# First projection of a hybrid decoder layer: squares on ScalarE, a weight split in front of the norm, one activation table for logarithm and exponent

## The chip, the cores and the metric

The kernel runs on one core of a Trainium2 chip. A core has five engines that work side by side, each with its own queue of instructions in a fixed order: TensorE (PE, matmuls, with its weight loads listed as PEld), VectorE (DVE), ScalarE (ACT), GpSimd (POOL) and SyncE (SP, which here issues most of the data transfers). They wait for each other through semaphores. The metric is the device time of one execution in microseconds.

## The reference, cut to what matters

One decoder layer over 512 positions of width 1024, in float32. The part that the change touches is the first line of work: the norm of the input and the combined input projection.

```
def rms_norm(x, g):
    xf = x.astype(jnp.float32)
    y = xf * lax.rsqrt(jnp.mean(xf * xf, axis=-1, keepdims=True) + NORM_EPS)
    return (y * g.astype(jnp.float32)).astype(x.dtype)
...
    h = rms_norm(x, norm_mix[l])
    proj = h @ w_in[l]
    hq, hf, hi, hg, mq, mk, mv = jnp.split(proj, IN_SPLITS, axis=-1)
    o_hgrn = hgrn2_mixer(hq, hf, hi, hg, lb_table[l], hgrn_norm[l])
```

The columns hf are the forget logits of a gated recurrence (f = lb + (1 - lb) sigmoid(hf), and its logarithm is summed up within chunks), hi its inputs, hq its queries, hg an output gate; mq, mk and mv feed a block-sparse attention. Behind this come an output projection, a cross-attention to 256 memory tokens, and an MLP with a squared ReLU, each with its norm and residual.

## The kernel before, in words

The activations lie transposed: 1024 features as eight slices of 128 partitions, 512 positions along the free axis. The weights come in units of 128x1024 (512 KB), numbered in the order of use. A unit is loaded by SP into a raw tile (wr; three such buffers, so that a load waits until an earlier unit has been split), and then split into two parts of reduced precision: the upper part wh is a copy on ACT, the lower part wl the difference on DVE (split_unit, L266 to L269). Each product is then three matmuls: upper by upper, upper by lower, lower by upper.

The norm is not applied to x in front of the projection. x is scaled by the gain alone and split (xhi on ACT, xlo on DVE, split_x), and the factor 1/rms, which depends on the position only, is multiplied into the results: rb1 holds it along the free axis, rc1 (made from rb1 by small matmuls, nc) per partition.

The stretch of the change, in the order of the code. First the loads of x and of the four units of the forget projection hf, mixed (L482 to L491). Then a tiny logarithm of eps on ACT (L517). Then, slice by slice as data arrive, split_w (the four units' columns), split_x and square_x(k). square_x squares slice k, on ACT for even k and on DVE for odd k, and DVE adds the squares up in Sx (slices 0 to 3) and Sy (4 to 7) and at last both in Sx. Slice 0 enters hf unsplit, as xg0, so its split comes last (split_x(0), L569); it is needed by the next stage, hi.

The projection hf (L626 to L640) runs over the slices, and within a slice over the four units, into four accumulator banks. Of the norm, norm_rows, three parts are hung into it: at slice 5 the sums are split for the column sum (nrh on ACT, nrl on DVE) and lower_bounds is issued, which needs one small exponent (lbv); at slice 6 two matmuls with ones give the column sum nr, ACT makes rb1 from it as exp(-0.5 ln(.)) (rsqrt_of), and split_unit() splits unit 4, the first unit of hi. Then ev_f empties each of the four banks on DVE (Fz = hf times rb1), ACT takes the sigmoid, DVE scales it. The stage hi uses the same four banks.

Two things set the order of instructions. Up to L642 (and from L1248 on) they run on each engine as they are written. Between these lines the Tile scheduler orders them, by its own estimate of when each is ready and by the order of the code; there the code itself also interleaves side work (the heads' recurrences and attentions) by a table of estimated times, the class Pace. The logarithm, the exponent and the sigmoid need an activation table on ACT; the compiler puts a load in front of each that needs another table than the one present. A line nc.scalar.preload_act_table_set(name) asks for a set by name; the MLP has one at L1178.

## Time and profile before

| | |
|---|---|
| time, median of 3 runs | 752.73 us (750.14, 752.73, 753.45) |
| the profiled execution | 749.8 us, its span 748.0 us, granted TensorE clock 0.996 |
| busy: PE, DVE, ACT | 734.2, 545.8, 415.3 us |
| hf stage on PE | 5.28 to 29.9 us after the start |
| first matmul of hi | 32.50 us after the start |

The span is the time from the first to the last instruction in the profile. Times in the profile's rows are microseconds after its start. Nearly all of the kernel's instructions are issued through one helper, so they carry the line L115; the names of the tiles tell them apart. A name on the left of an arrow is what an instruction writes, those on the right are what it reads. In a timeline a row gives the start, the duration, the engine, the operation, and, in brackets, how long the engine stood idle before it and what it waited for; "x2" means that neighbouring equal instructions are merged into one row.

### The profile page before, as it was taken

Reading aid. Unit: us, or ns where it says so; the run is one execution under the profiler, and the core shown is the slowest. Engines: PE = TensorE matmul, PEld = TensorE weight load, DVE = VectorE, ACT = ScalarE, POOL = GpSimd, SP = SyncE. Lnnn points to the kernel's source line nnn. Section 1 sums busy time; section 2 is a strip of 40 time slices with the busy share of each in tenths; the row PEclk is TensorE's granted clock in tenths of the full one; section 3 lists DMA queues with packets and bytes.
Section 4 is the critical chain, followed back from the end, with each engine's and each line's share of the span. In section 5 each row is a group of like instructions: output and inputs, shape, how many; then the busy total and the mean of one; then the engine's idle time right before and its main releaser. Section 6 shows DMA issues by size and latency. Waiting matters only on the chain.

```text
span 748.0 us, 11991 instructions
## 1 busy us (share of the span) xinstructions
PE 734.2 (98%) x4702; PEld 662.4 (89%) x4702; DVE 545.8 (73%) x894; ACT 415.3 (56%) x636; POOL 49.4 (7%) x62
## 2 busy tenths in 40 slices
PE   9899999999999999999999999999999999999995
PEld 6688888777787998888888999999999999999995
DVE  5799744877776646677468788787879778878783
ACT  6684547334665554455355655555556554546562
POOL 1000000000011210011001011222100000000000
PEclk9999999999999999999999999999999999999998
DMA  9134334534679897459826488899986655545631
GB/s 312 50 130 152 113 113 141 182 128 142 169 201 253 206 291 286 141 125 275 285 104 141 109 236 217 226 216 236 236 205 236 199 191 177 191 147 173 218 117 57
DMA packets 45321, 137.03 MB, mean 183 GB/s; under 512 B 4528, under 2 KB 8880, under 8 KB 44624
## 3 DMA queue, kind: packets, MB, share of 16 engines
q1 hardware_dynamic: 35824, 110.64, 43.4%
q0 software_dynamic: 8960, 25.17, 18.8%
q8 instruction: 37, 0.61, 0.3%
q10 hardware_dynamic: 480, 0.45, 0.2%
q14 instruction: 20, 0.16, 0.1%
HBM read 134.15 MB, written 35.65 MB: 227 GB/s over the span
## 4 chain that ended last, share of the span: by engine, by line
PE 93%; ACT 3%; DVE 2%; DMA 1%; issue 1%; SPq 0%; DVEq 0%; ACTq 0%
PE X L115 24%; PE Y L115 15%; PE xo L115 7%; PE mkq L115 6%; PE xq L115 6%; PE wo L115 5%; PE Z L115 3%; PE hi L115 3%; PE hg L115 3%; PE mv L115 3%; PE hq L115 3%; PE memv L115 3%; PE memk L115 2%; PE xs L115 2%; PE a L115 1%; PE sc L115 1%
## 5 line engine op out<-in xcount | busy, mean ns | idle before, releaser
L115 ACT ACTIVATE wh<-wr 128x1024 fp32r<-128x1024 f32 x120 | 125.8, 1055 | 114.2 <-PE X L115 16.9
L115 DVE TENSOR_TENSOR wl<-wr,wh 128x1024 fp32r<-128x1024 f32 x120 | 146.0, 1221 | 43.0 <-ACT wh L115 28.5
L115 PE MATMUL X<-op,wh 128*128 128x256 f32 x512 | 92.7, 284 | 0.0
L115 PEld LDWEIGHTS X<-op,wh 128*128 128x128 f32 x512 | 80.0, 192 | 0.1
L115 PE MATMUL X<-op,wl 128*128 128x256 f32 x256 | 72.8, 284 | 0.6 <-DVE wl L115 0.6
L200 POOL DMA_DIRECT2D u<-in_ws_dram x32 | 31.0, 967 | 328.3 <-DMA mraw<-in_memT_dram 191.0
L115 PEld LDWEIGHTS X<-op,wl 128*128 128x128 f32 x256 | 49.2, 192 | 0.8 <-DVE wl L115 0.8
L115 PE MATMUL Y<-OS,wh 128*128 128x256 f32 x256 | 47.2, 284 | 0.2 <-ACT t L115 0.2
L115 PE MATMUL X<-OS,wh 128*128 128x256 f32 x256 | 46.5, 284 | 0.0
L115 PE MATMUL Y<-op,wh 128*128 128x256 f32 x256 | 46.2, 283 | 0.0
L115 PEld LDWEIGHTS Y<-OS,wh 128*128 128x128 f32 x256 | 40.0, 192 | 0.5 <-ACT t L115 0.4
L115 PEld LDWEIGHTS Y<-op,wh 128*128 128x128 f32 x256 | 40.0, 192 | 0.0
L115 PEld LDWEIGHTS X<-OS,wh 128*128 128x128 f32 x256 | 39.9, 192 | 0.0
L115 PE MATMUL X<-OS,wl 128*128 128x256 f32 x128 | 36.3, 283 | 0.0
L115 PE MATMUL Y<-op,wl 128*128 128x256 f32 x128 | 36.3, 283 | 0.0
L115 PE MATMUL Y<-OS,wl 128*128 128x256 f32 x128 | 36.2, 283 | 0.0
L115 ACT ACTIVATE g<-t 128x512 f32<-128x512 f32 x32 | 19.0, 624 | 28.6 <-DVE t L115 28.6
L115 ACT ACTIVATE op<-g 128x1024 fp32r<-128x1024 f32 x28 | 29.2, 1044 | 0.5 <-PE X L115 0.5
L115 DVE TENSOR_TENSOR op<-g,op 128x1024 fp32r<-128x1024 f32 x24 | 29.2, 1218 | 0.0
L115 ACT ACT_TABLE_LOAD x22 | 28.2, 1283 | 1.5 <-PEq L1407 1.2
L115 PE MATMUL mkq<-xhi,wl 128*128 128x512 f32 x64 | 26.6, 416 | 0.0
L115 PE MATMUL mkq<-xhi,wh 128*128 128x512 f32 x64 | 26.5, 414 | 0.0
(319 smaller groups left out, 2103.9 us busy)
## 6 DMA issues: line engine op xcount, KB each, us to landing
wr<-in_ws_dram SPq DMA_DIRECT2D x88, 512.0 KB, 4.4
u<-in_ws_dram POOLq DMA_DIRECT2D x32, 512.0 KB, 7.6
wr<-u SPq DMA_DIRECT2D x32, 512.0 KB, 3.4
u<-in_ws_dram SPq DMA_DIRECT2D x16, 512.0 KB, 3.9
u<-u SPq DMA_DIRECT2D x16, 512.0 KB, 5.9
wA<-in_ws_dram SPq DMA_DIRECT2D x8, 512.0 KB, 7.3
wD<-in_ws_dram SPq DMA_DIRECT2D x8, 512.0 KB, 7.8
wB<-in_ws_dram SPq DMA_DIRECT2D x8, 512.0 KB, 3.9
```

Of the source, the lines that this page charges most:

```text
L115: return f(*args, **kw)
L200: return nc.gpsimd.dma_start(dst, src, accum_op=ALU.add, max_dma_last_dim=4 * D)
```

## The change

All eight squares of square_x are ACT activations now; the adds stay on DVE. A split_unit() is added behind the squares of slices 4 to 7 and in front of split_x(0): it splits unit 4 there. The split_unit() at slice 6 (L640) stays as it is, and so splits unit 5. The logarithm of eps is replaced by a request for the table set that holds both logarithm and exponent, at the same place.

```
-    A.activation(sink, eps, AF.Ln)
+    nc.scalar.preload_act_table_set("natural_log_exp_and_others")
...
-        if k % 2 == 0:
-            A.activation(q, src, AF.Square)
-        else:
-            V.tensor_mul(q, src, src)
+        A.activation(q, src, AF.Square)
         if k not in sums:
-            S, eng = (Sx, V) if k < 4 else (Sy, V)
-            eng.tensor_add(S, S, q)
+            S = Sx if k < 4 else Sy
+            V.tensor_add(S, S, q)
...
     for k in range(4, KT):
         square_x(k)
+    split_unit()
     split_x(0)
```

## Rows read from the trace of the kernel before

**Rows 1.** The page's first part: busy time of each engine, its share of the span, and its instructions.

```profile
PE 734.2 (98%) x4702; PEld 662.4 (89%) x4702; DVE 545.8 (73%) x894; ACT 415.3 (56%) x636; POOL 49.4 (7%) x62
```

**Rows 2.** Waits of TensorE in the execution, longest first; the three of the first 34 us that have to do with the norm and with hi: who waited for whom, microseconds in total, how often, the longest.

```profile
PE hi L115 <- ACT wh L115: 2.5, 1, 2.5
...
PE nr L115 <- ACT nrh L115: 0.3, 1, 0.3
...
PE nr L115 <- DVE nrl L115: 0.2, 1, 0.2
```

**Rows 3.** Timeline of TensorE, the two rows with a wait between 34 and 423 us.

```profile
235.87 0.61 PE L115 MATMUL nc<-ident,rbm 128*128 128x1 f32 x4 [0.65 <-ACT rbm L115]
...
422.27 0.50 PE L115 MATMUL Y<-OS,wh 128*128 128x256 f32 x2 [0.18 <-ACT t L115]
```

**Rows 4.** Timeline of TensorE and its weight loads, 25.5 to 34.4 us: the end of hf with the norm's column sum, and the start of hi.

```profile
25.51 0.39 PE L115 MATMUL hf<-xhi,w4l 128*128 128x512 f32 x1
26.18 0.48 PE L115 MATMUL nr<-nrh,ones_r 128*128 128x512 f32 x1 [0.28 <-ACT nrh L115]
26.81 0.50 PE L115 MATMUL nr<-nrl,ones_r 128*128 128x512 f32 x1 [0.16 <-DVE nrl L115]
27.15 0.40 PE L115 MATMUL hf<-xhi,w4h 128*128 128x512 f32 x1
...
29.66 0.39 PE L115 MATMUL hf<-xhi,w4l 128*128 128x512 f32 x1
32.50 0.88 PE L115 MATMUL hi<-wh,xhi 128*128 128x512 f32 x2 [2.45 <-ACT wh L115]
...
32.87 0.19 PEld L115 LDWEIGHTS hi<-wh,xhi 128*128 128x128 f32 x1 [0.19 <-DVE Fz L115]
```

**Rows 5.** Timeline of DVE, 26 to 34 us.

```profile
26.07 0.69 DVE L115 TENSOR_TENSOR nrl<-Sx,nrh 128x512 fp32r<-128x512 f32 x1
...
31.53 1.29 DVE L115 TENSOR_TENSOR Fz<-hf,rb 128x512 f32<-128x512 f32 x2 [3.17 <-ACT rb L115]
32.74 1.22 DVE L115 TENSOR_TENSOR wl<-wr,wh 128x1024 fp32r<-128x1024 f32 x1
```

**Rows 6.** Timeline of ACT, 25 to 34 us.

```profile
25.40 0.63 ACT L115 ACTIVATE nrh<-Sx 128x512 fp32r<-128x512 f32 x1 [6.22 <-DVE Sx L115]
26.05 1.28 ACT L115 ACT_TABLE_LOAD   x1
...
27.57 1.28 ACT L115 ACT_TABLE_LOAD   x1
...
29.57 1.28 ACT L115 ACT_TABLE_LOAD   x1
30.87 0.63 ACT L115 ACTIVATE rb<-rb 128x512 f32<-128x512 f32 x1
31.41 1.04 ACT L115 ACTIVATE wh<-wr 128x1024 fp32r<-128x1024 f32 x1
```

**Rows 7.** Timeline of DVE, a square with its add, and the first use of the constants.

```profile
12.64 0.69 DVE L115 TENSOR_TENSOR xsq<-xraw 128x512 f32<-128x512 f32 x1
13.43 0.69 DVE L115 TENSOR_TENSOR Sx<-Sx,xsq 128x512 f32<-128x512 f32 x1
...
72.47 2.69 DVE L115 COPY_PREDICATED AT<-cst,a 128x512 f32<-128x512 int32 x7
```

**Rows 8.** Timeline of ACT and of the transfers on its queue (ACTq), 11 to 19 us.

```profile
11.85 0.62 ACT L115 ACTIVATE Sx<-xraw 128x512 f32<-128x512 f32 x1
12.37 0.71 ACT L115 ACTIVATE xhi<-xraw,vec 128x512 fp32r<-128x512 f32 x1
...
16.29 0.33 ACTq L115 DMA_DIRECT2D cst<-in_consts_dram  x1
...
18.47 0.71 ACT L115 ACTIVATE xhi<-xraw,vec 128x512 fp32r<-128x512 f32 x1
```

**Rows 9.** The raw tile wr, instructions of 9 to 11 us: the loads of the first two units (duration of the issue in ns, first and last start), and the time from issue to landing.

```profile
L115 SPq DMA_DIRECT2D wr<-in_ws_dram x2: 340/340/340, 10.0 to 10.7; - x2
...
DMA to landing us min/median/max: 7.6/7.8/8.1
```

**Rows 10.** Timeline of SP's queue between 20 and 60 us: all that it issues there.

```profile
33.98 23.03 SPq L115 DMA_DIRECT2D wr<-in_ws_dram  x7
```

**Rows 11.** The stretch from 20 to 25 us: its length, busy time of PE, PEld, DVE, ACT and POOL (instructions), granted clock, share of the DMA engines that is busy, GB/s.

```profile
20.00:25.00 5.00, 5.00 (x24) 4.14 (x23) 4.72 (x8) 0.00 (x0) 0.00 (x0) 1.00 0.07 24
```

**Rows 12.** Timeline of ACT at the MLP's norm, behind the request of the same table set at L1178, and of TensorE and ACT at the end of the kernel.

```profile
423.81 1.28 ACT L1178 ACT_TABLE_LOAD   x1
...
426.07 0.67 ACT L115 ACTIVATE rb<-nr,eps 128x512 f32<-128x512 f32 x1
426.77 0.63 ACT L115 ACTIVATE rb<-rb 128x512 f32<-128x512 f32 x1
...
739.75 0.70 PE L115 MATMUL fs<-fsq,ones 128*128 128x256 f32 x2 [0.53 <-ACT fsq L115]
...
740.49 0.47 ACT L115 ACTIVATE rb<-fs,eps 128x256 f32<-128x256 f32 x1 [0.39 <-PE fs L115]
```

**Rows 13.** Timeline of ACT at the norm of the memory, 230 to 238 us.

```profile
230.63 1.06 ACT L115 ACTIVATE wh<-wr 128x1024 fp32r<-128x1024 f32 x1 [0.76 <-PE wo L115]
...
237.55 1.06 ACT L115 ACTIVATE wh<-wr 128x1024 fp32r<-128x1024 f32 x1 [1.21 <-PE wo L115]
```

## The prediction

> **What bounds the kernel now.** I read the busy shares first: TensorE (PE) is busy for 734.2 of 748.0 us, VectorE (DVE) and ScalarE (ACT) for 73% and 56% [rows 1]. So a change of the other two counts only where TensorE stands still for them, and the second view is TensorE's list of waits [rows 2]. Its largest entry, 2.5 us, is the first matmul of the input branch (hi) waiting for the split weight wh. Two smaller ones (0.3 and 0.2 us) are the column sums of the first norm (nr) waiting for the two halves of the summed squares. These three lie in the stretch that the diff touches; behind it, up to 423 us, there are two waits, 0.65 and 0.18 us [rows 3].

> The third view is the three engines' timeline from 20 to 36 us [rows 4 to 6], read backwards from the gap. Matmuls of the forget projection hf follow each other at 0.228 us (27.15 to 29.66 us, eleven steps). After the one at 29.66 the next could start at 29.89; it starts at 32.50, 2.61 us late. ACT ended wh at 32.45. ACT reached it at 31.41 because since 25.40 it had worked without a pause through: upper half of the sums (nrh), table load, a small exponent (lbv), table load, logarithm, table load, exponent (both into rb). And it began that at 25.40 because DVE had the sums Sx ready only then: ACT had stood idle for 6.22 us, while DVE squared and added. The same lateness shows on TensorE at nr: from 25.51 to 27.15 there are three steps, which at 0.228 take 0.68 us and took 1.64, so 0.96 us is lost. A last bit: the weights of hi's second matmul load 0.37 us after the first's (32.50, 32.87), held by the DVE product Fz that empties their bank, 0.14 us above a step [rows 4].

> **The change part by part.**
> *Four squares from DVE to ACT.* DVE loses four products. Two independent ones of this size take 1.29 us, 0.69 each and so 0.60 from start to start [rows 5]; a square starts 0.79 us before the add that needs it [rows 7]. So DVE gains 4 x 0.60 = 2.4 us at least, 4 x 0.79 = 3.2 at most. ACT gains four at 0.52 us from start to start [rows 8], 2.1 us. The first two push the operand splits in the ACT queue back by 0.5, then 1.0 us. TensorE takes 12 x 0.228 = 2.73 us for each of the eight slices, so slice 4 begins near 17.5 us (slice 6 ends at 25.51); its upper half is ready at 13.08 [rows 8]. The slack is over 4 us and the cost nothing. The other two lengthen ACT where it then sat idle for 6.2 us; the last square ends near 18.47 + 2.1 + 0.1 = 20.65.

> [...]

> *The split of unit 4 in front of the norm.* ACT runs wh after the last square, 20.55 to 21.6: its raw weights, issued at about 10.0, land at most 8.1 us later [rows 9], by 18.1. DVE runs wl (1.22 us) between the sum Sx and xlo of slice 0. Then the lower half nrl, which ended at 26.76, ends at 26.76 - 2.4 + 1.2 = 25.6 (24.8 with the 3.2). TensorE wants nrh at 25.74 and nrl at 25.97: both are there, and the 0.96 us goes. Queued behind this wl are xlo, nrl and the small lbv operations; the cover is 0.4 us, and beyond it every us of delay stops TensorE, as nr stands in its queue in front of slice 7. The call that stayed in slice 6 now splits unit 5, which TensorE needs one unit (24 matmuls, 5.5 us) later. On SP's queue the loads that wait for a free raw buffer, first issued at 33.98, move to about 24 us [rows 10], where the DMA engines are busy for 0.07 of their time or less [rows 11]: no cost. Three loads on ACT's queue (cst at 16.29 [rows 8] and two behind it) come up to 4 us later; cst is first read at 72.47 us [rows 7]. No cost.

> *One table set.* The loads at 26.05, 27.57 and 29.57 go, 1.28 us each, 3.85 us of ACT time [rows 6]. That one preload serves logarithm and exponent is seen at 423.81: load, logarithm, and the exponent 0.70 us behind the logarithm, with no room for a second load of 1.28 [rows 12]. The first load was there before (for the dropped logarithm of eps), so nothing is added at the start.

> *What is late next.* nr's second matmul starts at 25.97 and ends after 0.50 [rows 4]; ACT follows TensorE by 0.04 (740.45 to 740.49) [rows 12]: logarithm at 26.5, exponent at 27.2, done at 27.85. DVE's Fz follows after 0.03 as at 31.53 and takes 0.69: the first bank is free at 28.55, the second 0.6 later. TensorE, without the 0.96, ends slice 7's steps at 28.93 and can start hi at once: wh and wl are long there, the bank since 0.4 us. So the 2.61 goes as a whole, and the 0.14 with it, since six matmuls (1.4 us) now stand between two banks.

> *Sum.* 0.96 + 2.61 + 0.14 = 3.7 us, and hi starts at 28.9 instead of 32.50. Behind it TensorE has no gap to absorb this; ACT and DVE, which lose one weight split each from the crowded stretch after 30 us, are early by 3.6 us and more as well. Unknown is only the order: from the end of hf to the end of the cross-attention the Tile scheduler orders instructions by its own estimates, and those move with the change. Its effect is bounded by the waits: at best the 0.65 and the 0.18 us go too; at worst new waits of a few ACT instructions arise (below). I take zero, since the work in both orders is the same and TensorE hid it all but once.

> The profiled execution took 749.8 us, span 748.0. By the sum: span 744.3, time 746.1. The median of the runs shown is 752.73, 2.9 above that execution; the same 3.7 us off it give 749.0, which I predict.

> **Rivals.**
> *A: the split of unit 5 gets in front of Fz on DVE.* It is issued before Fz, and ends on ACT only after the norm's exponent: wh 27.75 to 28.8, wl to 30.0, first Fz to 30.7, so hi starts 1.8 us later than 28.93. Gain 1.9 us, 750.8 us. Against it: in the rows two Fz (31.53) ran ahead of such a wl (32.74) [rows 5]. For it: the scheduler decides by estimates, and there the split is the earlier instruction.

> *B: the reordering also closes the later waits* (0.65 and 0.18 us): gain 4.5 us, 748.2 us. For it: both are waits on ACT, which now runs ahead; against it: ACT's lead doesn't help where it waits for TensorE itself, only another order would.

> *C: the reordering makes a wait that costs more than the gain.* Place: the memory norm, where TensorE already waits for rbm [rows 3]. Each weight split wh that comes in front of rbm on ACT adds 1.06 us [rows 13]. It decides from four of them on (4.2 us against 3.7); with eight, 8.5 - 3.7 = 4.8 us slower, 757.5 us. For it: nothing but that the order is open; against it: two wh of that stretch are 6.9 us apart (230.63, 237.55), so that one more can be and eight hardly.

> *D: the loads don't go*, because the compiler places its own all the same. Then after lbv's exponent, about 26.2 (0.6 behind nrl's end), come load, logarithm, load, exponent and Fz: 1.28 + 0.67 + 1.28 + 0.63 + 0.69 with 0.1 between them, 30.9. hi starts 1.9 us late: gain 1.8 us, 750.9 us. Rows 12 speak against it.

> **How the numbers follow.** Forecast 0.62, A 0.16, B 0.12, C 0.05, D 0.05. The runs shown scatter from 750.14 to 753.45, 2.6 below and 0.7 above their median; I carry this over. Low end: between forecast and B, less 2.6: 746.0. High end: A and D with 0.7 to 0.9 above, 751.8. C is left out. Changes under 0.5% (3.76 us) can't be told from none here, and the forecast of 3.7 us lies on that edge: half of its chance is on each side. Faster by more: 0.31 + B 0.12 + a little for A and D where the median before was a high draw (its lowest run is 0.3% below it), 0.47. Within: 0.48. Slower by more than 0.5%: C, 0.05.

> **What would show it.** Right: the wait of hi on wh gone from TensorE's list, both nr waits too; hi's first matmul at 28.9 us after the start; three table loads fewer, none between nrh and the sigmoid's; the square products gone from DVE; ACT's 6.2 us of idle time before nrh cut to about 2. Wrong: hi's first matmul waiting for Fz beyond 0.4 us (A), loads still beside rb (D), or new lines in TensorE's waits after 34 us (C). If all the early steps hold and the span is still not 3 us or more shorter, the gain was given back later, and the sum's last step failed.

## The result and the profile after

| | before | after |
|---|---|---|
| time, median | 752.18 us (six runs, 750.14 to 753.45) | 746.63 us (six runs, five of them 746.31 to 747.69) |
| ratio after to before | | 0.9929, 95% interval 0.9912 to 0.9947 |
| the profiled execution, its span | 749.8, 748.0 us | 746.53, 744.8 us |
| first matmul of hi | 32.50 us | 29.17 us |

One execution of the changed kernel took 4018 us (it counts in the median of six; the other five have 746.59) and one of the kernel before, beside an experiment, 1470 us; the range, the ratio and all that follows leave both out. By the ratio the changed kernel is faster by 0.71%, 5.3 us of 752.18. The forecast was 749.0 us and a gain of 3.7 us: the time lies in the range, the two profiled executions differ by 3.3 us, but the medians differ by 5.5 us. Where the further 2 us come from is what the experiments had to find.

First the profile after, and in it the waits of TensorE, longest first; it answers to [rows 2].

```profile
PE warm L115 <- POOL eps L493: 1.0, 1, 1.0
PE nc L115 <- ACT rbm L115: 0.6, 1, 0.6
PE X L115 <- DVE wl L115: 0.6, 1, 0.6
PE fs L115 <- ACT fsq L115: 0.5, 1, 0.5
PE Y L115 <- ACT t L115: 0.2, 1, 0.2
```

This is the whole list. The wait of hi on wh and both waits of nr are gone; what is left was there before. (A wait of 0.3 us of hf on xlo, early on, is missing here too; it comes and goes between the kernels, and hf as a whole is no earlier here.) The timeline of TensorE after, 25 to 35 us, answers to [rows 4].

```profile
25.69 0.40 PE L115 MATMUL hf<-xhi,w4l 128*128 128x512 f32 x1
25.92 0.40 PE L115 MATMUL nr<-nrh,ones_r 128*128 128x512 f32 x1
26.16 0.40 PE L115 MATMUL nr<-nrl,ones_r 128*128 128x512 f32 x1
26.40 0.40 PE L115 MATMUL hf<-xhi,w4h 128*128 128x512 f32 x1
...
28.94 0.39 PE L115 MATMUL hf<-xhi,w4l 128*128 128x512 f32 x1
29.17 0.39 PE L115 MATMUL hi<-wh,xhi 128*128 128x512 f32 x1
29.40 0.39 PE L115 MATMUL hi<-wl,xhi 128*128 128x512 f32 x1
...
33.76 0.95 PE L115 MATMUL nc<-ident,rb 128*128 128x1 f32 x8
```

From slice 6 through nr and slice 7 into hi the matmuls start 0.23 to 0.24 us apart, without a break. The timeline of ACT after, 20 to 30 us, shows why; it answers to [rows 6].

```profile
20.72 1.05 ACT L115 ACTIVATE wh<-wr 128x1024 fp32r<-128x1024 f32 x1
21.66 0.72 ACT L115 ACTIVATE xhi<-xraw,vec 128x512 fp32r<-128x512 f32 x1
23.31 0.63 ACT L115 ACTIVATE nrh<-Sx 128x512 fp32r<-128x512 f32 x1 [0.93 <-DVE Sx L115]
26.05 0.21 ACT L115 ACTIVATE lbv<-lbv 128x8 f32<-128x8 f32 x1 [2.11 <-DVE lbv L115]
26.66 0.69 ACT L115 ACTIVATE rb<-nr,eps 128x512 f32<-128x512 f32 x1 [0.40 <-PE nr L115]
27.38 0.63 ACT L115 ACTIVATE rb<-rb 128x512 f32<-128x512 f32 x1
27.92 1.04 ACT L115 ACTIVATE wh<-wr 128x1024 fp32r<-128x1024 f32 x1
28.98 1.28 ACT L115 ACT_TABLE_LOAD   x1
```

No load stands between nrh (23.31) and the sigmoid's (28.98), the 6.22 us of idle time in front of nrh are 0.93, and the logarithm waits for nr, that is for TensorE, and no longer the other way round. DVE after, in its timeline, answers to [rows 5]: nrl is done at 25.68, and the two Fz run ahead of the split of unit 5.

```profile
24.99 0.69 DVE L115 TENSOR_TENSOR nrl<-Sx,nrh 128x512 fp32r<-128x512 f32 x1
...
28.05 1.29 DVE L115 TENSOR_TENSOR Fz<-hf,rb 128x512 f32<-128x512 f32 x2 [0.98 <-ACT rb L115]
29.25 1.22 DVE L115 TENSOR_TENSOR wl<-wr,wh 128x1024 fp32r<-128x1024 f32 x1
```

So the path went as worked out. What the path doesn't explain is why the unprofiled executions of the kernel before took 2.4 us longer than the profiled one, and those of the changed kernel not.

### The profile page after: what moved, and what is told of

Its sections match the earlier page's. It is cut to its first block, busy times and chain, and to the rows that moved or that the text cites. A ratio compares the mean times of both kernels' runs of the same rounds, so it can differ in the third digit from the quotient of the medians.

```text
span 744.8 us, 11989 instructions
## 1 busy us (share of the span) xinstructions
PE 734.2 (99%) x4702; PEld 662.8 (89%) x4702; DVE 543.6 (73%) x890; ACT 413.4 (56%) x636; POOL 49.4 (7%) x62
## 4 chain that ended last, share of the span: by engine, by line
PE 97%; ACT 1%; DVE 1%; issue 0%; DVEq 0%; POOL 0%; ACTq 0%; POOLq 0%
PE X L115 24%; PE Y L115 15%; PE xo L115 7%; PE mkq L115 6%; PE xq L115 6%; PE wo L115 5%; PE hf L115 3%; PE Z L115 3%; PE hg L115 3%; PE mv L115 3%; PE hq L115 3%; PE memv L115 3%; PE hi L115 3%; PE memk L115 2%; PE xs L115 2%; PE a L115 1%
## 5 line engine op out<-in xcount | busy, mean ns | idle before, releaser
L115 PEld LDWEIGHTS Y<-OS,wh 128*128 128x128 f32 x256 | 39.9, 192 | 0.5 <-ACT t L115 0.4
L115 PEld LDWEIGHTS Y<-op,wh 128*128 128x128 f32 x256 | 39.9, 192 | 0.0
L115 PEld LDWEIGHTS X<-OS,wh 128*128 128x128 f32 x256 | 39.9, 192 | 0.0
L115 ACT ACTIVATE g<-t 128x512 f32<-128x512 f32 x32 | 19.0, 625 | 29.6 <-DVE t L115 29.6
L115 ACT ACTIVATE op<-g 128x1024 fp32r<-128x1024 f32 x28 | 29.2, 1044 | 0.5 <-PE X L115 0.5
L115 PE MATMUL mkq<-xlo,wh 128*128 128x512 f32 x64 | 26.5, 414 | 0.0
L115 PE MATMUL mkq<-xhi,wh 128*128 128x512 f32 x64 | 26.5, 414 | 0.0
```

The costliest lines, as they stand in the source:

```text
L115: return f(*args, **kw)
```

## The experiments

Theories. *Path:* the time follows the start of hi; the 2 us are scatter of the runs drawn. *Order:* the 2 us come from the new order of instructions behind hf, which the split brings. (In the traces, compared by tile names behind 28 us, ACT and DVE differ from the kernel before in 26 stretches with the whole change, in 24 with the split alone, in three to five in the three kernels squares, table, and both, which lack the split, and in two between two profiles of the kernel before itself.) A third one, *clock*, was formed after the first seven runs. Every kernel ran beside the kernel before on the same chip. These executions of the kernel before, 61 on three chips, fall in three groups: 12 at 749.7 to 750.5 us, 25 at 750.9 to 752.0, and 24 at 752.4 to 753.7. All experiments in one table; the start of hi is that of the profiled execution, the clock the lowest and highest mean granted clock of the runs, each over its whole execution.

| kernel | hi starts, us | runs, us: lowest, median, highest | clock | ratio, 95% interval |
|---|---|---|---|---|
| squares | 30.32 | 747.68, 748.0, 749.27 | 0.994 to 0.997 | 0.9957 (0.994 to 0.9973) |
| split | 33.39 | 750.53, 751.45, 752.8 | 0.995 to 0.998 | 0.9998 (0.9986 to 1.0011) |
| table | 30.16 | 746.95, 747.44, 747.62 | 0.996 to 0.998 | 0.9944 (0.9929 to 0.9959) |
| squares, table | 29.50 | 746.03, 746.74, 747.17 | 0.996 to 0.997 | 0.9934 (0.9919 to 0.995) |
| split, table | 30.86 | 747.82, 748.44, 750.11 | 0.996 to 0.998 | 0.996 (0.9945 to 0.9976) |
| squares, split | 31.04 | 748.16, 748.95, 749.22 | 0.996 to 0.998 | 0.9964 (0.9951 to 0.9977) |
| before again | 32.58 | 751.58, 753.13, 753.7 | 0.992 to 0.994 | 1.0012 (0.9999 to 1.0025) |
| before, gap filled | 33.62 | 750.33, 750.98, 751.3 | 0.996 to 0.998 | 0.9983 (0.9974 to 0.9992) |
| after, gap of 8 copies | 34.21 | 751.85, 752.8, 753.97 | 0.991 to 0.996 | 1.001 (0.9998 to 1.0022) |
| after, gap of 4 copies | 31.35 | 747.78, 748.3, 749.92 | 0.994 to 0.998 | 0.9953 (0.9937 to 0.9969) |
| after again | 28.52 | 745.99, 746.55, 747.03 | 0.996 to 0.997 | 0.9927 (0.9912 to 0.9941) |

### Each part alone

**Squares alone.**

```
-        if k % 2 == 0:
-            A.activation(q, src, AF.Square)
-        else:
-            V.tensor_mul(q, src, src)
+        A.activation(q, src, AF.Square)
```

> Squares alone (all eight on ACT, no other edit). Path theory: the sums are ready 2 us earlier and both nr waits go, but the three table loads stay between nrh and wh: logarithm near 26.8, second load to 28.8, exponent to 29.4, wh to 30.4; hi starts near 30.4 us instead of 32.50, gain 2.1 us, ratio 0.997. Order theory (the 2 us that the unprofiled runs gained beyond the profiled one come from the new order behind hf, which only the split brings): the same, 0.997. Rival that the squares cost ACT time which TensorE waits for: a new wait on xhi or w4h before 25 us, ratio 1.000 or more.

hi started at 30.32 as the path said, and no wait on xhi or w4h was added. But the ratio is 0.9957, a gain of 3.7 us for a start 2.2 us earlier.

**Split alone.**

```
         square_x(k)
+    split_unit()
     split_x(0)
```

> Split in front of the norm alone. Path theory: wl (1.2 us) delays nrl to about 27.9 us, TensorE stands 1.1 us longer at nr, slice 7 ends near 31.0; the loads stay, rb near 31.1, the first Fz to 31.8, so hi starts at 31.9: gain 0.6 us, ratio 0.999. Order theory: 2 us more, ratio 0.9965.

Nothing was gained: 0.9998. The price in front of nr is as worked out. The timeline of TensorE with the split alone shows nrl's matmul waiting behind the wl that now stands ahead of nrl on DVE.

```profile
26.49 0.47 PE L115 MATMUL nr<-nrh,ones_r 128*128 128x512 f32 x1 [0.27 <-ACT nrh L115]
28.14 0.50 PE L115 MATMUL nr<-nrl,ones_r 128*128 128x512 f32 x1 [1.18 <-DVE nrl L115]
...
33.39 0.50 PE L115 MATMUL hi<-wh,xhi 128*128 128x512 f32 x1 [2.04 <-DVE Fz L115]
```

The start of hi I had 1.5 us too early (31.9 against 33.39): lbv's inputs come behind wl as well, so lbv runs at 28.46 and the logarithm's load only after it. As hi starts 0.9 us later than in the kernel before, the path would make this kernel slower by 0.9 us, 1.001; it is as fast as before. So some part of the 2 us may be in it too, and this run decides nothing between the theories.

**One table set alone.**

```
-    A.activation(sink, eps, AF.Ln)
+    nc.scalar.preload_act_table_set("natural_log_exp_and_others")
```

> One table set alone. Path theory: nr is as late as before (26.81), but rb is ready at 28.7 instead of 31.5 and wh at 29.6; hi starts at 29.9 with slice 7's end: gain 2.6 us, ratio 0.9965; the waits of nr stay. Order theory: the same 0.9965, as the order behind hf stays that of before.

hi started at 30.16, near the 29.9 expected, the waits of nr stayed. The timeline of TensorE at the start of hi:

```profile
30.16 0.77 PE L115 MATMUL hi<-wh,xhi 128*128 128x512 f32 x2
30.77 0.95 PE L115 MATMUL nc<-ident,rb 128*128 128x1 f32 x8
31.57 0.49 PE L115 MATMUL hi<-wl,xhi 128*128 128x512 f32 x1
```

The ratio is 0.9944, some 4.3 us in the medians for a start 2.3 us earlier: again 2 us more than the path gives, without the split and, but for those few stretches, with the old order behind hf. The order theory falls. This one line alone brings four fifths of what the whole change brings.

### Two parts at a time

**Squares and table**, the diffs of both, no split.

> Squares and one table set, without the split. Path theory: nr on time (26.2), rb near 28.0, wh behind it by 29.0, just before slice 7 ends; wl comes behind two Fz at 30.5, covered by the first two matmuls of hi and the eight of nc; hi starts near 29.2 as with all three: gain 3.3 us, ratio 0.9955, so the split adds nothing. Order theory: 0.9955 too, but then 2 us (0.0026) above the whole change, which stands at 0.9929. Split theory (the split is what frees hi): hi late by 1 us or more, ratio 0.997.

0.9934, beside 0.9929 and 0.9927 of the whole change: no difference. The split adds nothing here. TensorE's timeline shows how the lower part comes in time without it.

```profile
29.50 0.72 PE L115 MATMUL hi<-wh,xhi 128*128 128x512 f32 x2
30.06 0.95 PE L115 MATMUL nc<-ident,rb 128*128 128x1 f32 x8
30.86 0.48 PE L115 MATMUL hi<-wl,xhi 128*128 128x512 f32 x1
```

wl of unit 4 ended at 30.80 on DVE (29.58 and 1.22 us); two matmuls of hi that don't need it and nc cover the time until then.

**Split and table.**

> Split and one table set, the squares as before. Path theory: nrl near 27.9, slice 7 ends at 31.0, rb at 30.0, first Fz to 30.7: hi starts near 31.0, gain 1.5 us, ratio 0.998. Order theory: 2 us more, 0.9953.

0.996: worse than the table alone (0.9944) by about 1 us in the medians; its lowest run (747.82) lies above the highest of the table alone (747.62). nr waits 1.2 us for nrl as with the split alone. The ratio is again better than the path's 0.998.

**Squares and split**, the logarithm of eps as before.

> Squares and split, the logarithm of eps as before (so the three loads stay). Path theory: nr on time, lbv near 26.1, load, logarithm, load, exponent to 30.2, Fz to 30.9: hi starts near 30.9, gain 1.6 us, ratio 0.998. Order theory: 2 us more, 0.995.

hi started at 31.04 behind a wait of 1.7 us for Fz, as worked out for rival D (30.9). The row of TensorE's timeline:

```profile
31.04 0.50 PE L115 MATMUL hi<-wh,xhi 128*128 128x512 f32 x1 [1.68 <-DVE Fz L115]
```

The ratio 0.9964 is no better than the squares alone (0.9957). With loads beside rb the split frees nothing, since rb and with it Fz and the bank come later than wh.

### The kernel before, once more

> The kernel before, unchanged, against itself. If the gain beyond the profiled 3.2 us was a matter of the runs that happened to be drawn: ratio 1.000 with an interval of 0.002 or less, the runs all within 750 to 753.5, and the profiled one anywhere among them. If the profiled execution is a different kind of execution than the timed ones (749.8 against a median of 752.2): its profile again near 749.8 and the runs near 752.

This settles where to look. The profiled execution was 753.28 us this time, span 751.5. Up to hi it is that of before (hi at 32.58). TensorE's timeline goes on otherwise:

```profile
32.58 1.10 PE L115 MATMUL hi<-wh,xhi 128*128 128x512 f32 x2 [2.47 <-ACT wh L115]
33.48 1.70 PE L115 MATMUL nc<-ident,rb 128*128 128x1 f32 x8
...
35.61 0.63 PE L115 MATMUL hi<-wh,xlo 128*128 128x512 f32 x1
36.04 0.63 PE L115 MATMUL hi<-wh,xhi 128*128 128x512 f32 x1
...
39.88 0.41 PE L115 MATMUL hi<-wl,xhi 128*128 128x512 f32 x1
40.12 0.39 PE L115 MATMUL hi<-wh,xlo 128*128 128x512 f32 x1
```

Matmuls of hi start 0.43 us apart until 39.9 us, and only then 0.23. The windows say why. Columns: stretch, its length, busy time (instructions) of PE, PEld, DVE, ACT, POOL, granted TensorE clock, DMA share, GB/s.

```profile
28.00:30.00 2.00, 2.00 (x10) 1.42 (x8) 0.38 (x3) 1.97 (x3) 0.00 (x0) 1.00 0.00 0
30.00:32.00 2.00, 0.11 (x1) 0.00 (x0) 0.39 (x1) 1.99 (x3) 0.00 (x0) 1.00 0.00 0
32.00:34.00 2.00, 1.42 (x6) 1.14 (x6) 2.00 (x4) 1.97 (x3) 0.00 (x0) 0.77 0.02 4
34.00:36.00 2.00, 2.00 (x8) 1.85 (x9) 2.00 (x5) 2.00 (x4) 0.00 (x0) 0.50 0.46 141
36.00:38.00 2.00, 2.00 (x6) 1.57 (x5) 2.00 (x4) 2.00 (x4) 0.00 (x0) 0.50 0.30 121
38.00:40.00 2.00, 2.00 (x6) 1.52 (x6) 2.00 (x4) 1.98 (x2) 0.00 (x0) 0.53 0.58 156
40.00:42.00 2.00, 2.00 (x11) 1.60 (x10) 0.62 (x1) 1.99 (x2) 0.00 (x0) 1.00 0.88 281
```

Behind the gap the granted clock falls to half (0.50 from 34 to 38 us). The next stage, hq, starts at 58.75 us here and at 55.45 in the first profile of before, where the clock stayed at 1.00 from 20 to 740 us: 3.3 us. (At the end of the kernel, behind the last matmul, it falls to 0.50 as well, from 741.9 us on in the first profile of before and from 740.7 us on in that of the changed kernel; no matmul is slowed by that, but it pulls the mean clock down, to 0.996 and 0.997 in these two.) That is the third theory: *the gap costs its length, and in most executions also a stretch at half clock behind it.* The first profile was of one that escaped.

The runs agree. In the 61 executions of before above the mean granted clock is 0.996 in the group at 749.7 to 750.5 us, 0.994 to 0.995 in the middle one, 0.992 to 0.993 in the one at 752.4 to 753.7. The twelve of before again add none to the first group, four to the second and eight to the third. With the squares alone the profile shows the intermediate case, behind a gap of 1.0 us (windows, the same columns).

```profile
30.00:32.60 2.60, 2.28 (x13) 1.95 (x14) 2.60 (x5) 2.57 (x4) 0.00 (x0) 1.00 0.00 0
32.60:36.20 3.60, 3.60 (x10) 2.79 (x9) 3.60 (x6) 3.60 (x6) 0.00 (x0) 0.53 0.41 148
36.20:38.00 1.80, 1.80 (x9) 1.48 (x9) 1.80 (x4) 1.77 (x3) 0.00 (x0) 1.00 0.68 237
```

0.53 over 3.6 us is 0.50 for 3.4 us. The split alone has one such stretch in its profile, behind its wait of 2.0 us (33.9 to 37.3 us; windows, the same columns).

```profile
34.00:36.00 2.00, 2.00 (x6) 1.57 (x5) 2.00 (x3) 1.99 (x4) 0.00 (x0) 0.50 0.00 0
36.00:38.00 2.00, 2.00 (x7) 1.58 (x7) 2.00 (x5) 2.00 (x4) 0.00 (x0) 0.68 0.79 262
```

In stretches of 0.2 us, 17 lie below 0.75 with the squares alone and with the split alone, and 34 in the profile of before again: 3.4 and 6.8 us. At half clock, with matmuls 0.43 us apart for 0.23, these lose by my estimate about half their length, 1.7 and 3.4 us, close to the distances between the groups (medians 749.93, 751.71 and 753.04 us: 1.8 and 3.1).

Set against the lowest group of before, 749.93 us, the gains are close to what the earlier start of hi gives: squares, in its four runs at 748.2 us or less, 2.1 us (hi 2.2 earlier), table 2.5 (2.3), squares and table 3.2 (3.0), split and table 1.5 (1.6), squares and split 1.0 (1.5), the whole change 3.3 (3.3).

Two things don't fit so well. In the split alone the mean clock doesn't sort the runs (750.53 us at 0.995, 751.42 at 0.998); the end of the kernel is in it, but whether that is why no profile shows. And one execution of the changed kernel, 747.69 us, has a mean clock of 0.946 and is only 1.1 us slower than the others; no profile shows why.

### Filling the gap, and opening it again

**The kernel before, its gap filled** with work for nothing: eleven matmuls into a bank that is not read, and nc behind them.

```
+    fill = side_bank("fill")
+    for i in range(11):
+        nc.tensor.matmul(fill, ones_r, xhi[0][:, 1, :], start=True, stop=True, skip_group_check=True)
+    for _ in norm_x:
+        pass
     Fz = s8(F32, "Fz")
```

> The kernel before, with 11 matmuls whose result nobody reads (128x512, 0.23 us each) on TensorE between hf and hi, over the gap of 2.5 us, and nc right behind them. Clock theory (the gap lets the granted clock fall to 0.5 for some us in most executions): hi ends its last matmul as late as in the profile of before with full clock (55.2 us, 55.5 with a wait on wl), but now in every run: granted clock 1.00 from 28 to 42 us, all runs at 749.6 to 750.6 us, ratio 0.9975, although 2.5 us of work were added. Rival (the scatter of before comes from elsewhere, the gap costs only its length): runs from 749.7 to 753.6 as before, ratio 1.000.

```profile
30.25 2.72 PE L643 MATMUL fill<-xhi,ones_r 128*128 128x512 f32 x11
32.81 0.95 PE L115 MATMUL nc<-ident,rb 128*128 128x1 f32 x8
33.62 0.48 PE L115 MATMUL hi<-wh,xhi 128*128 128x512 f32 x1
34.36 0.50 PE L115 MATMUL hi<-wl,xhi 128*128 128x512 f32 x1 [0.26 <-DVE wl L115]
```

TensorE's timeline above: hi starts 1.1 us later than before. All the same the kernel is faster than before, 0.9983 with an interval below 1, no run has a mean clock under 0.996, and the twelve runs lie within 1.0 us instead of 4. In its profile the granted clock is 1.00 from 28 to 42 us. The median is 0.4 us above the upper end of what I gave: hq starts at 56.00, 0.55 us later than in the first profile of before, and a later matmul waits 0.4 us for DVE (a on qx), which it doesn't do there. So the groups come from the gap, and their price from the clock. The edit also moves nc in front of hi; that nc stands there too in the next experiment, where the lower clock comes back, says that the move isn't what keeps the clock up.

**The changed kernel, its gap opened again** by eight copies on ACT whose results nobody reads.

```
         elif k == NORM_AT:
+            for i in range(8):
+                nc.scalar.activation(xg0, xraw[0][:, 0, :], AF.Copy)
             next(norm_x)
```

> The changed kernel with 8 useless copies (128x512, 0.52 us each) on ACT in front of the norm's logarithm, so that TensorE has its gap back: rb near 31.8, nc behind it, hi near 32.7 instead of 29.17, of which 0.9 us is nc moved to the front: 2.7 us later. Path theory alone: all runs near 749.3, ratio 0.9965. Clock theory: part of the runs there, most 1.5 to 3 us above it with a lower mean clock, in two or three groups; median 751 to 752, ratio 0.999 to 1.000.

```profile
32.48 1.87 PE L115 MATMUL nc<-ident,rb 128*128 128x1 f32 x8 [3.74 <-ACT rb L115]
34.21 0.77 PE L115 MATMUL hi<-wh,xhi 128*128 128x512 f32 x1
34.78 0.63 PE L115 MATMUL hi<-wl,xhi 128*128 128x512 f32 x1
```

The gap came out longer than meant, 3.7 us, so the path alone gives 746.6 + 5.0 (hi at 34.21) - 0.9 (nc in front of it) less what the half clock took from nc (0.9, its 1.87 against 0.95): near 749.8, or 750.3 with the wait of 0.5 us of a on qx that is new here too. No run came near that: six lie at 751.9 to 752.4 and six at 753.2 to 754.0, their clock at 0.996 to 0.991. The medians of the two halves, 752.3 and 753.6, lie 1.9 and 3.3 us above 750.3, about one and two stretches at half clock; the profile, of a run in the upper half, has 0.50 from 32.5 to 39.3 us. All three parts of the change are in place, and the gain is gone.

**The same with four copies.**

> The same with 4 copies: rb near 29.7, TensorE idle for 0.6 us and then on nc, hi near 30.6, 0.5 us later than in the changed kernel net of nc. Path theory: all runs near 747.2. Clock theory with a threshold on the idle time: the same 747.2, no lower clock; if the eight small matmuls of nc count as idle time too: some runs at 748 to 749 with a lower clock, as with the squares alone (1.0 us of gap).

TensorE was idle for 0.7 us in front of nc. Five runs lie at 747.8 to 748.3, 0.6 to 1.1 us above my figure (0.5 of it is the wait of a on qx, which is here too), with the clock at 0.996 or more, and one at 749.92 with 0.994. One run of six is thin, but it has the clock of the middle group, and it agrees with two of six for the squares alone (749.21 and 749.27 at 0.994 to 0.995). So a gap of 0.7 to 1.0 us, next to nc's small matmuls, can be enough; for 0.7 us that rests on one run without a profile. Against it stand squares and split: their gap is 1.7 us, nc comes later there, and none of nine runs has a time or a clock (0.996 to 0.998) that says half clock, nor has the profile, with 1.00 from 28 to 42 us. So the length of the gap alone doesn't decide. That nc counts as idle time would fit, but it was not tried by itself.

**The changed kernel again.**

> The changed kernel again, beside the others on one chip. Clock theory: no gap in the stretch, so no groups: all runs within 746.2 to 747.2, mean clock 0.997 in each, ratio 0.993.

745.99 to 747.03, clock 0.996 to 0.997, as expected but for 0.2 us at the lower end.

## Why the prediction was right, and which term was too small

*The bound and the reading of the gap* were right: 0.96 us at nr, 2.61 in front of hi, and the chain from Sx to wh behind both.

*Squares.* DVE's gain was as taken: nrl was done at 25.68 (I had 25.6). No split was late for TensorE. Each of the eight squares takes 0.62 us on ACT in the profile after, the product on DVE took 0.69 [rows 7]. One reading was loose: slice 0, which enters unsplit, takes 3.4 us on TensorE (5.28 to 8.68) and not 2.73; nothing hung on it.

*Split in front of the norm.* Its price (1.2 us ahead of nrl) and its cover were right. What I hadn't asked is whether it is needed: squares and table reach the same time without it (0.9934), and it costs about 1 us where the squares stay on DVE and the table set is one (0.996 against 0.9944).

*One table set.* Right: the logarithm at 26.66 (26.5), rb done at 28.01 (27.85), the first bank free at 28.74 (28.55). The three loads are gone, 21 instead of 24 in all.

*What is late next.* hi at 29.17 instead of 28.93: the whole hf stage ran 0.2 us later in this execution (slice 6 ends with the matmul at 25.69, before at 25.51). In the profile of after again hi starts at 28.52, 0.4 us earlier than I had it, so this stage varies by some tenths between executions. The bank was free 0.4 us ahead, as said.

*Rivals.* A fell: Fz ran ahead of wl. B fell: the 0.65 and the 0.18 us are still in the list. C fell: the order behind hf changed (26 stretches on ACT and DVE) and made no new wait of TensorE. D fell in the change itself; squares and split without the preload showed its mechanism, at 31.04 for the 30.9 that I gave.

*The sum* holds for the profiled executions (3.3 us of time, 3.7 forecast) and is too small by 2 us for the median. The term that failed is the 2.61 us: I priced the gap at its length at full clock, from the one execution that showed full clock, and the 749.0 came from taking the same 3.7 us off a median that was 2.9 us (with all six runs 2.4 us) above that execution. I saw that difference and carried it over as scatter. It was no scatter without a cause: of 61 executions of the kernel before 49, by their times and mean clocks, paid a further 1.8 or 3.1 us of half clock behind the gap, 12 x 0 + 25 x 1.8 + 24 x 3.1 over 61 is 2.0 us on average. 3.3 + 2.0 gives 5.3, as the ratio does; the medians differ by 5.5. That is also why the changed kernel's runs lie so close together: the low end of the range, 746.0, was set by a scatter that they don't have, and the time fell above it by 0.6 us. The range held the time, but not for the reason given, and in part by luck: the path's 3.3 us alone are 0.44%; beyond the edge of 0.5%, on which the prediction had put itself, the change came only by the cost that it hadn't seen.

## What to carry to other kernels

Price a gap on TensorE by its length and by what follows it; here that was 2.5 us and, in 49 of 61 executions by their times and mean clocks, a further 1.8 or 3.1 us of half clock. So look at the granted clock in windows behind each gap, and when the profiled execution is among the lowest of the runs, take a second profile before calling the difference scatter. The chain that held up TensorE was best shortened at the loads and waits in it (squares and table 0.9934, the whole change 0.9929); work moved in front of the chain (here the split) brought nothing even where the rest was short, and cost about 1 us where the squares stayed behind (0.996 against 0.9944). Here one line, the table set, alone brought four fifths (0.9944).

## What the runs showed of the hardware that was not expected

No run here shows what decides it: how long TensorE has to stand idle, or why behind the same gap one execution of a kernel runs at 0.50 and another at 1.00.
